# Pacing side work by measured prices, gate rows over 128 partitions, and a first norm at fixed places of TensorE's order

## The chip, the cores and the metric

The kernel runs on one core of a Trainium2 chip. A core has a matrix engine (TensorE, "PE" in the profile, with its weight loads as "PEld"), a vector engine (VectorE, "DVE"), a scalar engine (ScalarE, "ACT"), a general engine (GpSimd, "POOL") and an engine that here only issues transfers (SyncE, "SP"). Each runs its own queue of instructions in the order in which the compiled program has them, and waits on the others by semaphores. The metric is the device time of one execution in microseconds (us), as a median of several.

## The reference

One inference step of one layer of a hybrid decoder, in fp32, for 256 prompt tokens and 8 cached single-token requests ("sample" tokens), 264 columns in all. Cut to what matters:

```python
def layer(x, ...):                                  # D_MODEL 2048
    xn = rmsnorm(x, g_mix)
    z = xn @ w_in                                   # x part and gate part of rg, q, k, v, o, two gate rows per head
    # recurrent group (rg): conv, two block-diagonal gates, linear scan, gelu gate, norm
    xr, conv_new = causal_conv(z[..., :1024], ...)
    r, ig = sigmoid(block_diag(xr, ...)), sigmoid(block_diag(xr, ...))
    log_a = -8.0 * r * softplus(-lam)
    h = associative_scan(a = exp(log_a), bx = sqrt(1 - exp(2 * log_a)) * ig * xr)
    y_rg = rmsnorm(h * gelu(z_gate), g_rg_out)
    # mLSTM group: 4 heads, dk 128, dv 256, input gate logi and forget gate logf per head and token
    h_ml, C_new, n_new, m_new = mlstm(q, k, v, logi, logf, C0, n0, m0)
    y_ml = rmsnorm(h_ml, g_ml_out) * sigmoid(z_o)
    x = x + concat([y_rg, y_ml]) @ w_out
    # cross attention: 4 heads of 512 over 256 memory tokens
    xq = rmsnorm(x, g_xa) @ w_xa_q
    x = x + (softmax(xq @ mk.T * 512 ** -0.5) @ mv) @ w_xa_o
    xf = rmsnorm(x, g_ffn)                          # SwiGLU, 5632 wide
    return x + (silu(xf @ w_ffn_gate) * (xf @ w_ffn_up)) @ w_ffn_down
```

The prompt's memory keys and values are computed here from a normalised memory; the 8 sample tokens each have their own cached keys and values and their own mLSTM state, which are read from memory, used and, for the state, written back. The outputs are the normalised activations and all new states.

## The kernel before

Tokens lie along the free dimension (264 columns), features on the 128 partitions in chunks. The big products are made in three single-pass matmuls per chunk: activations and weights are each split into a high part in a rounded format and a remainder, and high x high, high x low and low x high are summed (`mm3`). The weights come in pieces of 2048 columns; each piece is one *step* of PE, 48 matmuls of 128x264. A list `steps` holds them in order: 0 to 3 the first bank pass over the input projection, 4 to 7 the rest of rg's x part, 8 the gate rows (`pe_if`), 9 to 16 q and k, 17 to 24 v, 25 to 32 rg's gate part, 33 to 40 o, 41 to 56 `w_out`, 57 to 72 `w_q`, 73 to 104 memory keys and values head by head, 105 to 120 `w_o`, then the feed-forward part. Each step has a source, a matmul function, an evacuation function and a list of names that it needs.

For every step the weights are split by a copy on ACT and a subtraction on DVE, per half of 1024 columns (`split_half`); four split buffers hold two steps, so a split starts when the matmuls of two steps earlier have read their half. The PSUM banks for the steps' results are four ("mm"), and four others ("ax") serve everything else.

All other work (norms, the rg recurrence, the mLSTM, the cached attention) is written as Python generators that are emitted between steps. The loop over the steps (before: lines 1299 to 1343) emits in this order: at some steps the end of a generator is forced (`finish`); the evacuation of the step before (`pend`), at raised priority; the split of the next step's weights; the step's matmuls; and then side generators through `pump(pe.clock + SLACK)`, SLACK being 0.5. The engines are wrapped in an object that adds a price to a clock for every instruction emitted (`price_dve`, `price_act`, `price_pe`, lines 64 to 77). `pump` lets a generator emit as long as the priced DVE and ACT clocks are both below the limit; a generator yields after small portions, and `yield STEP` gives up its turn for this step. A generator of priority below zero is run to its end with high priority. So the prices decide how much side work stands between two steps on each engine. A scheduler of the language then settles the final order on each engine, apart from stretches that are marked as manual.

Names that the change and the prediction touch:

- `norm_x`, the first norm's sums, reciprocal root and spreading over the partitions; `rstd` is its result. Before, it is a side generator of priority -1 that is started after step 3; its end is forced before step 5, and the result of step 4 stays unevacuated until then.
- `rg_gen` (from line 479): the recurrence; before it is started ahead of step 5.
- `evac_if` and `ml_gates` (lines 575 to 638): the gate rows of four heads, on partitions 0 to 3 of seven row tiles `R(0)` to `R(6)`. Their sums and maxima are spread over all partitions by matmuls against columns of the identity, `ident[0:4, h:h+1]`; five blocks of 128 columns are transposed.
- `ml_prompt` (from 665): the decay matrix of each head, which starts with one such spreading matmul over 256 columns.
- `ml_sample` (from 754): the state update of the sample tokens in 32 groups (4 heads, 8 requests): two ACT copies, one DVE `scalar_tensor_tensor` of 128x256 and two of 128x128 that accumulate. `bcs` holds its factors.
- `evac_o` (856): evacuation of the o steps, which forces `ml_sample` and the heads to their end; `ml_norm` (820) makes the mLSTM's norm.
- `rg_out` (541): norm and split of rg's result. `mem_gen`: the memory norm and its split.
- the cached attention ("dk" and "dv", 32 pairs of a key and a value tile): per pair three dot products on DVE, a sum over partitions by way of POOL and PE, an Exp, and four accumulating products on DVE. The first `w_o` step needs them, and the attention of head 2, finished.

Of the kernel before, what the change touches and what calls it, by code (L numbers as in the profile page):

```python
# [17 lines left out]
P = 128  # L18
D = 2048
KC = D // P  # L20
T = 256
# [42 lines left out]
def price_dve(name, n, a, k):  # L64
    fast = name in ("tensor_scalar", "tensor_copy", "tensor_single_scalar", "memset")
    if name == "tensor_reduce":
        n = int(np.prod(a[1].shape[1:]))
    return 0.07 + n * (0.00052 if fast else 0.0066 if name == "reciprocal" else 0.00104)


def price_act(name, n, a, k):
    return 0.12 + n * 0.00083


def price_pe(name, n, a, k):
    passes = 1 if name == "transpose" or a[1].dtype == F32R else 4
    return passes * n * 0.00042 + 0.003


@with_exitstack  # L80
def layer_kernel(ctx: ExitStack, tc, xT, memT, vec, wrg, w_in, w_out, w_q, w_k, w_v, w_o,
# [150 lines left out]
    def mm3(ps, a, b, start, stop):  # L232
        ah, al = a
        bh, bl = b
        pe.matmul(ps, ah, bh, start=start, stop=False)
        pe.matmul(ps, ah, bl, start=False, stop=False)
        pe.matmul(ps, al, bh, start=False, stop=stop)
# [20 lines left out]
    def side(g, prio=0):  # L258
        x = Gen(g, prio)
        gens.append(x)  # L260
        gens.sort(key=lambda q: q.prio)
        return x
# [12 lines left out]
    def finish(cond):  # L275

        for _ in range(10000):
            if cond():
                return
            pump(1e12)  # L280
        raise RuntimeError("side work does not end")
# [293 lines left out]
    def evac_if(ps):  # L575
        R = Arr(7)
        ml["R"] = R
        li, u, a, b = (R(j)[0:4] for j in range(4))
        act.activation(a, ps[64:68, :N], AF.Copy)
        act.activation(b, ps[96:100, :N], AF.Copy)  # L580
        dve.tensor_add(li, ps[0:4, :N], a)
        dve.tensor_add(u, ps[32:36, :N], b)
        dve.tensor_mul(li, li, rstd[0:4, :])
        dve.tensor_mul(u, u, rstd[0:4, :])
        dve.tensor_scalar(li, li, V("bi")[0:4], None, op0=OP.add)
        dve.tensor_scalar(u, u, V("bf")[0:4], None, op0=OP.add)
        ml["gates"] = side(ml_gates(), 1)
# [6 lines left out]
    def ml_gates():  # L594
        R = ml["R"]
        li, u, e, lf, b, g, M = (R(j)[0:4] for j in range(7))
        yield STEP
        dve.scalar_tensor_tensor(e, u, -1.0, u, op0=OP.mult, op1=OP.min)
        act.activation(e, e, AF.Exp)
        yield 0.4  # L600
        log1p(lf, e)
        yield 6.0
        dve.tensor_scalar(u, u, 0.0, None, op0=OP.min)
        dve.tensor_sub(lf, u, lf)

        one = ones[0:4, 0:1].to_broadcast([4, T])
        dve.tensor_tensor_scan(b[:, :T], one, lf[:, :T], 0.0, op0=OP.mult, op1=OP.add)
        dve.tensor_sub(g[:, :T], li[:, :T], b[:, :T])
        dve.tensor_tensor_scan(M[:, :T], g[:, :T], g[:, :T], 0.0, op0=OP.max, op1=OP.max)
        dve.tensor_add(b[:, :T], b[:, :T], M[:, :T])  # L610
        dve.tensor_scalar(M[:, :T], M[:, :T], -1.0, None, op0=OP.mult)
        dve.tensor_copy(mrow[:, 0:1], b[:, T - 1: T])

        s = slice(T, N)
        dve.tensor_add(lf[:, s], lf[:, s], V("m0", 0, 8)[0:4])
        dve.tensor_max(b[:, s], lf[:, s], li[:, s])
        dve.tensor_copy(mrow[:, 1:], b[:, s])
        x16 = e[:, 0:16]
        dve.tensor_sub(x16[:, 0:8], lf[:, s], b[:, s])
        dve.tensor_sub(x16[:, 8:16], li[:, s], b[:, s])  # L620
        act.activation(x16, x16, AF.Exp)
        pool_e.dma_start(o_m, mrow)
        yield 3.0
        yield STEP
        yield STEP
        ps = bank("ax")
        for h in range(H):
            pe.matmul(ps[:, h * 16: h * 16 + 16], ident[0:4, h: h + 1].to_broadcast([4, P]), x16,
                      start=True, stop=True)
        i4 = ident[0:4, 0:4]  # L630
        for j in range(2):
            pe.transpose(ps[:, 64 + 4 * j: 68 + 4 * j], g[:, j * P: j * P + P], i4)
        for j, w0 in enumerate(WIN):
            pe.transpose(ps[:, 72 + 4 * j: 76 + 4 * j], b[:, w0: w0 + P], i4)
        act.activation(bcs, ps[:, 0:64].rearrange("p (h j) -> p h j", j=16), AF.Copy)
        act.activation(gcol, ps[:, 64:72].rearrange("p (j h) -> p j h", h=H), AF.Copy)
        act.activation(emc, ps[:, 72:84], AF.Exp, scale=-1.0)
        yield 0.1
# [26 lines left out]
    def ml_prompt():  # L665
        qk = ml["qk"]
        yield STEP
        kt = B([P, 2, H, P])
        for tb in range(2):
            ps = bank("ax")  # L670
            for h in range(H):
                pe.transpose(ps[:, h * P: h * P + P], qk(4 + h)[:, tb * P: tb * P + P], ident)
            act.activation(kt[:, tb].rearrange("p h d -> p (h d)"), ps, AF.Copy)
            yield STEP
        while "gates" not in ml or not ml["gates"].done:
            yield STEP
        R = ml["R"]
        M = R(6)[0:4, :T]
        for h in range(H):
            sel = ident[0:4, h: h + 1].to_broadcast([4, P])  # L680
            bc = bank("ax")
            pe.matmul(bc[:, :T], sel, M, start=True, stop=True)
            sps = bank("ax")
            q, k = qk(h), qk(4 + h)
            pe.matmul(sps[:, 0:256], k[:, 0:P], q[:, 0:T], start=True, stop=True)
            pe.matmul(sps[:, 256:384], k[:, P:T], q[:, P:T], start=True, stop=True)
            w = B([P, 1024])
            E, Pm, kw = w[:, 0:384], w[:, 384:768], w[:, 768:1024]
            ml["w", h] = (Pm, kw)
            yield STEP  # L690
            dve.tensor_scalar(E[:, 0:256], bc[:, 0:T], gcol[:, 0, h: h + 1], 0.0, op0=OP.add, op1=OP.min)
            dve.tensor_scalar(E[:, 256:384], bc[:, P:T], gcol[:, 1, h: h + 1], 0.0, op0=OP.add, op1=OP.min)
            act.activation(E, E, AF.Exp)
            dve.tensor_mul(E[:, 0:128], E[:, 0:128], mask)
            dve.tensor_mul(E[:, 256:384], E[:, 256:384], mask)
            dve.tensor_mul(Pm, sps[:, 0:384], E)
            act.activation(kw[:, 0:P], kt[:, 0, h, :], AF.Copy, scale=E[:, 255:256])
            act.activation(kw[:, P:T], kt[:, 1, h, :], AF.Copy, scale=E[:, 383:384])
            yield 1.0
            ml["pn"] = h + 1  # L700
# [167 lines left out]
    def proj(src, rhs, evac, cols=2048, n=N, need=()):  # L868

        def f(i):  # L870
            ps = bank()
            w = W(i)
            nch = cols // P
            for c in range(nch):
                mm3(ps[:, :n], w(c), rhs(c), c == 0, c == nch - 1)
            return ps
        steps.append((src, cols, f, evac, need))
# [418 lines left out]
        split_half(0, 1)  # L1296

    pend = []
    for i, (src, cols, pef, evf, need) in enumerate(steps):
        if i > 1:  # L1300
            load_piece(i + LD - 1)
        if i == 5:
            finish(lambda: fn.done)
            st["rg"] = side(rg_gen(), 0)
        for q in need:
            if q in st:
                finish(lambda: st[q].done)
        if i != 4:
            with tc.high_priority(300):
                for e, x in pend:  # L1310
                    e(x)
            pend = []
        now = pe.clock
        dve.clock, act.clock = max(dve.clock, now), max(act.clock, now)
        split_half(i + LS, 0)
        if i + LS < len(steps) and steps[i + LS][1] > 1024:
            split_half(i + LS, 1)
        ps = pef(i)
        if 1 <= i < 4:
            with tc.issue_after(st["split"].ins):  # L1320
                for c in range(4 * i if i > 1 else 0, 4 * i + 4):
                    sumsq(acc_x, xres[:, c, :], c == 0)
        if i == 3:
            fn = side(norm_x(), -1)
        if evf is not None:
            pend.append((evf, ps))
        if i == 0:
            for c in range(0, 4, 2):
                load_x(sp, 12 + c, 14 + c)
                load_first(3, c)  # L1330
                load_first(3, c + 1)
        else:
            load_piece(i + LD)
        pump(pe.clock + SLACK)
        if i == 24:
            ml["ng"] = side(ml_norm(), 6)
        if i == 40:
            st["memg"] = side(mem_gen(), 7)
# [113 lines left out]
```

## Time and profile before

| | us |
|---|---|
| median of 3 runs | 1552.53 (1551.74 to 1553.06) |
| span of the profiled execution | 1548.1 |
| PE busy in it | 1533.5 (99%) |
| DVE busy | 1055.5 (68%) |
| ACT busy | 784.0 (51%) |
| POOL busy | 123.7 (8%) |

The page of the profile gives for one execution the busy time of each engine, the chain of work that ended last, and groups of instructions. A group's row has line, engine, operation, output and inputs, sizes, count, then busy time and the mean of one in ns, and the idle time ahead of them with what ended it. Line 60 is the wrapper through which every engine call goes, so most rows carry L60 and are told apart by their tiles: `w` are split weights, `raw` the loaded ones, `mm` and `ax` PSUM banks, `t`, `lt` and `B` work tiles. In a timeline a row is the start, the duration of a run of like instructions, the engine, and in brackets the idle time before it and what released it; runs overlap a little because matmuls are pipelined. In a table by windows, each window has the busy time and count of each engine, then the granted TensorE clock as a fraction, the share of the transfer engines and GB/s.

### The profile page before, as it was taken

To read this page: it belongs to the slowest core of one execution; us is meant where nothing else is said; L and a number is where in the kernel's file an instruction comes from. 1 tells how busy PE (TensorE), PEld (TensorE's weight loads), DVE (VectorE), ACT (ScalarE), POOL (GpSimd) and SP (SyncE) were. 2 spreads that over 40 slices of the span, in tenths; PEclk is the share of its full clock that TensorE was granted. 3 is DMA by queue.
4 is the path that set the end of the run, shared out by engine and by line. 5 is a ranking of instruction groups with operands and counts; after the bars stand their busy time and mean duration, and the time that the engine had idled before them with its cause. 6 is when DMAs were issued, how large, how long until landed. Compare 5 with 4: busy or idle time off the path is not lost.

```text
span 1548.1 us, 30188 instructions
## 1 busy us (share of the span) xinstructions
PE 1533.5 (99%) x12098; PEld 1500.4 (97%) x12098; DVE 1055.5 (68%) x2026; ACT 784.0 (51%) x1255; POOL 123.7 (8%) x190
## 2 busy tenths in 40 slices
PE   9999999999999999999999999999999999999997
PEld 9999999999999888899999999999999999999997
DVE  7886888796699989876665555445555545555554
ACT  7565775665455656555444444333444433444463
POOL 0001210000134333310000000000000000000000
PEclk9999999999999999999999999999999999999999
DMA  9556984547789887855555555555555555555563
GB/s 301 187 164 204 309 288 171 193 158 259 251 294 356 320 296 252 309 181 180 187 177 181 186 181 188 181 185 183 183 185 181 186 183 186 180 188 178 163 181 107
DMA packets 99757, 326.01 MB, mean 211 GB/s; under 512 B 10945, under 2 KB 19825, under 8 KB 99617
## 3 DMA queue, kind: packets, MB, share of 16 engines
q1 hardware_dynamic: 83472, 269.57, 52.1%
q0 software_dynamic: 15136, 53.16, 9.7%
q8 instruction: 94, 1.54, 0.4%
q10 hardware_dynamic: 1008, 1.36, 0.3%
q14 instruction: 47, 0.38, 0.1%
HBM read 312.78 MB, written 11.28 MB: 209 GB/s over the span
## 4 chain that ended last, share of the span: by engine, by line
PE 96%; DVE 2%; ACT 1%; DMA 0%; issue 0%; SPq 0%; DVEq 0%; ACTq 0%
PE mm L60 90%; PE ax L60 6%; DVE B L60 1%; ACT B L60 0%; DVE w L60 0%; DMA raw<-w_in 0%; ACT w L60 0%; ACT L60 0%; DVE xres L60 0%; DVE c L60 0%; ACT rstd L60 0%; SPq L1278 0%; DVE acc_x L60 0%; DVEq L1429 0%; ACT t L60 0%
## 5 line engine op out<-in xcount | busy, mean ns | idle before, releaser
L60 PE MATMUL mm<-B,w 128*128 128x264 f32 (+1 forms) x10960 | 1365.3, 285 | 4.1 <-DVE w L60 2.4
L60 PEld LDWEIGHTS mm<-B,w 128*128 128x128 f32 x10960 | 1338.6, 188 | 16.4 <-DVE w L60 2.8
L60 ACT ACTIVATE w<-raw 128x1024 fp32r<-128x1024 f32 (+1 forms) x522 | 537.9, 1031 | 654.6 <-PE mm L60 447.3
L60 DVE TENSOR_TENSOR w<-raw,w 128x1024 fp32r<-128x1024 f32 (+1 forms) x522 | 623.1, 1195 | 357.0 <-ACT w L60 356.0
L60 PE MATMUL mm<-w,B 128*128 128x512 f32 x384 | 91.0, 391 | 0.0
L60 PEld LDWEIGHTS mm<-w,B 128*128 128x128 f32 x384 | 70.7, 188 | 14.3
L60 DVE TENSOR_TENSOR t<-mm,rstd 128x264 f32<-128x264 f32 x104 | 44.8, 431 | 44.2 <-PE mm L60 43.5
L1344 POOL TENSOR_TENSOR B<-B,rstd 128x264 f32<-128x264 f32 x4 | 2.8, 736 | 855.5 <-ACT rstd L60 855.5
L60 DVE TENSOR_TENSOR xres<-xres,mm 128x264 f32<-128x264 f32 (+1 forms) x81 | 34.2, 423 | 38.9 <-PE mm L60 38.9
L60 DVE SCALAR_TENSOR_TENSOR B<-B,dw 128x256 f32<-128x256 f32 x128 | 55.6, 488 | 3.9 <-ACT dw L60 3.9
L60 DVE SCALAR_TENSOR_TENSOR dw<-B,qsm,dw 128x256 f32<-128x256 f32 x96 | 49.6, 525 | 0.4
L60 PE MATMUL ax<-B,B 128*128 128x256 f32 (+3 forms) x288 | 48.1, 308 | 0.0
L60 PEld LDWEIGHTS ax<-B,B 128*128 128x128 f32 x288 | 40.8, 190 | 3.2 <-ACT w L60 0.3
L1031 POOL TENSOR_TENSOR ds<-dw,ds 128x256 fp32r<-128x256 f32 x32 | 34.6, 1085 | 108.1 <-ACT ds L60 108.1
L60 ACT ACTIVATE B<-xres,vecs 128x264 fp32r<-128x264 f32 (+1 forms) x64 | 32.1, 502 | 1.5 <-DVE xres L60 1.0
L60 ACT ACTIVATE t<-xres 128x264 f32<-128x264 f32 (+2 forms) x61 | 24.0, 410 | 15.2 <-DVE xres L60 15.2
L1020 POOL DMA_DIRECT2D B<-kcT x32 | 17.3, 542 | 140.1 <-DVE B L60 131.0
L60 ACT ACTIVATE B<-t 128x264 fp32r<-128x264 f32 (+1 forms) x60 | 24.2, 409 | 4.6 <-DVE t L60 4.3
L60 DVE TENSOR_TENSOR acc_x<-acc_x,t 128x264 f32<-128x264 f32 x59 | 25.1, 426 | 1.0 <-ACT t L60 0.5
L60 DVE SCALAR_TENSOR_TENSOR B<-xres,vecs,B 128x264 fp32r<-128x264 f32 x48 | 23.4, 487 | 3.1 <-ACT B L60 3.1
L60 ACT ACTIVATE t<-t 128x264 f32<-128x264 f32 (+1 forms) x61 | 24.8, 406 | 1.3 <-DVE t L60 1.2
L60 ACT ACTIVATE dw<-B,qsm 128x256 f32<-128x256 f32 x32 | 16.2, 507 | 17.4 <-DVE B L60 10.7
(152 smaller groups left out, 666.9 us busy)
## 6 DMA issues: line engine op xcount, KB each, us to landing
raw<-w_gu SPq DMA_DIRECT2D x176, 512.0 KB, 3.5
raw<-w_d SPq DMA_DIRECT2D x80, 512.0 KB, 3.5
raw<-w_in SPq DMA_DIRECT2D x74, 512.0 KB, 4.6
raw<-w_out SPq DMA_DIRECT2D x32, 512.0 KB, 4.0
B<-kcT POOLq DMA_DIRECT2D x32, 512.0 KB, 8.1
raw<-w_q SPq DMA_DIRECT2D x32, 512.0 KB, 3.7
B<-vcT POOLq DMA_DIRECT2D x32, 512.0 KB, 8.5
raw<-w_k SPq DMA_DIRECT2D x32, 512.0 KB, 6.8
```

Of the source, the lines that this page charges most:

```text
L60: return f(*a, **k)
L1020: pool_e.dma_start(kc, kcT[h, b])
L1031: pool_e.tensor_sub(ws[:, 1], acc, ws[:, 0].bitcast(F32))
L1344: e.tensor_mul(st["y"](c), st["y"](c), r)
```

## The change

Three parts. The prices become dearer and finer: a DVE instruction gets a fixed 0.15 or 0.21 us instead of 0.07 and more if it accumulates or scans, an ACT one 0.18 or 0.27 instead of 0.12 and more if it accumulates, a PE transpose and a small matmul their own fixed figures. The gate rows are used over all 128 partitions: two of the row tiles are set to zero first, the identity's whole column stands where four rows of it stood, and five transposes become matmuls against four columns of the identity. The first norm no longer is a side generator: its two parts are emitted at the third chunk of steps 5 and 6, PE's order is manual from step 4 to the end of step 6, the results of steps 4 to 6 stay unevacuated until step 7, and `rg_gen` starts at step 7.

```diff
-    return 0.07 + n * (0.00052 if fast else 0.0066 if name == "reciprocal" else 0.00104)
+    rate = {"reciprocal": 0.0066, "tensor_tensor_scan": 0.00208}.get(name, 0.00052 if fast else 0.00104)
+    fixed = 0.21 if name == "scalar_tensor_tensor" else 0.15
+    return fixed + n * rate + (0.08 if "accum_out" in k else 0.0)

 def price_act(name, n, a, k):
-    return 0.12 + n * 0.00083
+    by_column = not isinstance(k.get("scale", 1.0), (int, float))
+    return (0.27 if by_column else 0.18) + n * 0.00085 + (0.2 if "accum_out" in k else 0.0)

 def price_pe(name, n, a, k):
-    passes = 1 if name == "transpose" or a[1].dtype == F32R else 4
-    return passes * n * 0.00042 + 0.003
+    if name == "transpose":
+        return 0.11
+    if a[1].dtype == F32R:
+        return 0.0045 + n * 0.000437
+    return max(0.224, 0.005 + n * 0.00167)
...
     def evac_if(ps):
         R = Arr(7)
         ml["R"] = R
+        for q in range(2):
+            pool_e.memset(R.tile(q), 0.0)
...
         for h in range(H):
-            pe.matmul(ps[:, h * 16: h * 16 + 16], ident[0:4, h: h + 1].to_broadcast([4, P]), x16,
+            pe.matmul(ps[:, h * 16: h * 16 + 16], ident[:, h: h + 1].to_broadcast([P, P]), R(2)[:, 0:16],
                       start=True, stop=True)
-        i4 = ident[0:4, 0:4]
-        for j in range(2):
-            pe.transpose(ps[:, 64 + 4 * j: 68 + 4 * j], g[:, j * P: j * P + P], i4)
-        for j, w0 in enumerate(WIN):
-            pe.transpose(ps[:, 72 + 4 * j: 76 + 4 * j], b[:, w0: w0 + P], i4)
+        for o, x, at in ((64, R(5), WIN[:2]), (72, R(4), WIN)):
+            for j, w0 in enumerate(at):
+                pe.matmul(ps[:, o + 4 * j: o + 4 * j + 4], x[:, w0: w0 + P], ident[:, 0:4], start=True, stop=True)
...
-        M = R(6)[0:4, :T]
+        M = R(6)[:, :T]
         for h in range(H):
-            sel = ident[0:4, h: h + 1].to_broadcast([4, P])
+            sel = ident[:, h: h + 1].to_broadcast([P, P])
...
             for c in range(nch):
+                if i in (5, 6) and c == 2:
+                    with tc.high_priority():
+                        st["rstd_x"].run(lambda: True)
                 mm3(ps[:, :n], w(c), rhs(c), c == 0, c == nch - 1)
...
+    kept = ExitStack()
     for i, (src, cols, pef, evf, need) in enumerate(steps):
...
-        if i == 5:
-            finish(lambda: fn.done)
+        if i == 7:
             st["rg"] = side(rg_gen(), 0)
...
-        if i != 4:
+        if not 4 <= i < 7:
             with tc.high_priority(300):
                 for e, x in pend:
                     e(x)
...
+        if i == 4:
+            kept.enter_context(tc.manual_schedule(engines={mybir.EngineType.PE}))
         ps = pef(i)
+        if i == 6:
+            kept.close()
...
         if i == 3:
-            fn = side(norm_x(), -1)
+            st["rstd_x"] = Gen(norm_x())
```

## The prediction

> **What bounds the kernel now.** I read the page first, then TensorE's (PE's) waits, then its timeline around each wait, the granted clock there, and last the groups of VectorE (DVE) and ScalarE (ACT).
>
> ```profile
> PE 1533.5 (99%) x12098; PEld 1500.4 (97%) x12098; DVE 1055.5 (68%) x2026; ACT 784.0 (51%) x1255; POOL 123.7 (8%) x190
> PE 96%; DVE 2%; ACT 1%; DMA 0%; issue 0%; SPq 0%; DVEq 0%; ACTq 0%
> ```
>
> PE is busy for all but 14.6 of 1548.1 us and is 96% of the chain that ended last. So no pacing of DVE and ACT work can bring more than PE's few waits, and any work of theirs that becomes late is paid in full. The page's execution spans 1548.1 us; the median of the runs, 1552.53, lies 4.4 above it, and I add that constant to whatever I sum.
>
> ```profile
> PE mm L60 <- DVE w L60: 2.4, 2, 1.5
> PE mm L60 <- DVE B L60: 1.7, 1, 1.7
> ```
>
> ```profile
> 48.07 0.73 PE L60 MATMUL ax<-ident,c 128*128 128x128 f32 x6
> 48.66 0.73 PE L60 MATMUL mm<-B,w 128*128 128x264 f32 x4
> 51.12 12.00 PE L60 MATMUL mm<-B,w 128*128 128x264 f32 x98 [1.73 <-DVE B L60]
> ...
> 119.18 0.81 PE L60 MATMUL ax<-ident,B 4*128 4x4 f32 x5
> 121.52 8.68 PE L60 MATMUL mm<-B,w 128*128 128x264 f32 x57 [1.53 <-DVE w L60]
> ...
> 258.35 59.42 PE L60 MATMUL mm<-B,w 128*128 128x264 f32 x494
> ...
> 344.91 5.32 PE L60 MATMUL mm<-B,w 128*128 128x264 f32 x42 [0.82 <-DVE w L60]
> ```
>
> ```profile
> 118.00:122.00 4.00, 2.47 (x20) 2.05 (x20) 4.00 (x9) 3.60 (x7) 0.00 (x0) 1.00 0.01 2
> 122.00:126.00 4.00, 4.00 (x23) 4.00 (x22) 4.00 (x6) 0.61 (x2) 0.00 (x0) 0.57 0.59 180
> ```
>
> The three waits are 1.73 (first norm), 1.53 (recurrent block, "rg") and 0.82 us (memory norm). The windows (their seventh number is the granted clock) show what the second one drags behind it: 0.57 from 122 to 126 us, about 3.4 us at half speed. 57 matmuls take 8.68 us there; at 59.42/494 = 0.120 us each they would take 6.9, so about 1.7 us go to the clock.
>
> **First norm (steps 4 to 7).** The factor's work is fixed inside steps 5 and 6, and the results of steps 4 to 6 are scaled only before step 7.
>
> ```profile
> 49.26 1.31 DVE L60 TENSOR_TENSOR B<-ax,rstd 128x256 f32<-128x256 f32 x6 [2.03 <-ACT rstd L60]
> 50.48 0.89 DVE L60 TENSOR_TENSOR B<-mm,rstd 128x256 f32<-128x256 f32 x4
> ```
>
> Before, PE spreads the factor over the partitions at 48.07, because its place is there, and scaling ends at 51.37 (50.48 + 0.89), 3.3 us later; step 7, ready for its first matmul at 49.39, waits for it. In the changed order the spread stands within step 6, some 4 us earlier, so scaling ends near 47.3, 2 us before it is needed. The wait goes: -1.7 (0 if the factor's small DVE work in between takes 2 us longer). Next to be late are the weight splits of steps 8 to 10, which I count 1 to 2 us ahead. rg starting two steps later costs nothing by itself; what it pushes along is summed below.
>
> **Gate rows over 128 partitions.** Two POOL memsets are added; POOL is busy 8% and they stand a step ahead of their readers: nothing.
>
> ```profile
> 117.52 0.51 PE L60 MATMUL mm<-B,w 128*128 128x264 f32 x2
> 117.96 0.61 PE L60 MATMUL ax<-B,ident 4*128 4x16 f32 x4
> 118.42 0.38 PE L60 MATMUL ax<-ident,B 4*128 4x4 f32 x4
> ...
> 150.51 0.69 PE L60 MATMUL ax<-B,ident 4*128 4x256 f32 x2
> 151.14 0.92 PE L60 MATMUL ax<-B,B 128*128 128x256 f32 x4
> 151.89 0.60 PE L60 MATMUL ax<-ident,B 128*128 128x128 f32 x4
> ...
> 167.22 1.47 PE L60 MATMUL ax<-B,B 128*128 128x256 f32 x8
> 168.45 2.40 PE L60 MATMUL mm<-B,w 128*128 128x264 f32 x18
> ```
>
> From 150.51 to 151.89 are 1.38 us for one broadcast from 4 rows (256 columns) and a full-height pair (256 and 128 columns). Two such pairs alone take 167.22 to 168.45, 1.23 us, so 0.62 a pair and, at two thirds of it, 0.41 for 256 columns: 1.03 in all. By starts 0.35 is the price of four rows; by ends, where the matmul behind also loses some, I get 0.385. Four heads: -1.5. In the cluster at 117 to 120 the same happens at each change of height: two weight matmuls take 117.52 to 117.96, 0.44 instead of 0.24. Over its three changes that makes 0.6 to save, and five transposes that become matmuls of two passes cost about as much: nothing. Together -1.5 (0 to -2.3).
>
> [...]
>
> **Prices.** Side generators run until their priced DVE and ACT time passes PE's, and what is unfinished is forced out where a step needs it. Dearer prices on DVE and ACT mean fewer side instructions a step. That is good at 120 us (the 29-instruction rg block ahead of a split is broken up: -1.5 for the wait, -1.7 for the clock) and leaves the work of the cached tokens unfinished at two forced ends. I followed the changed program's order on each engine to both.
>
> ```profile
> L60 DVE TENSOR_TENSOR w<-raw,w 128x1024 fp32r<-128x1024 f32 x488 | 599.8, 1230 | 352.7 <-ACT w L60 351.8
> L60 DVE SCALAR_TENSOR_TENSOR B<-B,dw 128x256 f32<-128x256 f32 x128 | 55.6, 488 | 3.9 <-ACT dw L60 3.9
> L60 DVE SCALAR_TENSOR_TENSOR dw<-B,qsm,dw 128x256 f32<-128x256 f32 x96 | 49.6, 525 | 0.4
> L60 DVE TENSOR_TENSOR acc_x<-acc_x,t 128x264 f32<-128x264 f32 x59 | 25.1, 426 | 1.0 <-ACT t L60 0.5
> L60 DVE TENSOR_REDUCE dw<-ax 128x1 f32<-128x256 f32 x32 | 13.2, 415 | 2.5 <-PE ax L60 2.4
> L60 DVE DVE_READ_ACCUMULATOR B<-B,dw 128x1 f32 x128 | 10.0, 78 | 0.0
> ```
>
> ```profile
> L60 ACT ACT_TABLE_LOAD x12 | 15.4, 1283 | 2.8 <-issue 2.2 <-DVE t L60 0.4
> L60 ACT ACTIVATE w<-raw 128x1024 fp32r<-128x1024 f32 x488 | 516.7, 1060 | 640.4 <-PE mm L60 436.2 <-issue 189.7 <-ACT B L60 10.0
> L60 ACT ACTIVATE dw<-ax,dw 128x256 f32<-128x256 f32 x32 | 15.0, 470 | 13.4 <-DVE dw L60 13.2 <-POOL ds L1031 0.2
> L60 ACT ACTIVATION_READ_ACCUMULATOR dw<-ax,dw 128x1 f32 x32 | 6.3, 197 | 0.0
> ```
>
> *Forced end 1, behind step 37 (about 250 us).* The mLSTM state update of the cached tokens is 32 groups, one 128x256 and two accumulating 128x128 operations each.
>
> ```profile
> L60 DVE SCALAR_TENSOR_TENSOR B<-B,bcs,t x32: 470/478/485, 147.6 to 220.7; 128x256 f32<-128x256 f32 x32
> ```
>
> ```profile
> 207.83 0.48 DVE L60 SCALAR_TENSOR_TENSOR B<-B,bcs,t 128x256 f32<-128x256 f32 x1
> ...
> 208.89 1.22 DVE L60 TENSOR_TENSOR w<-raw,w 128x1024 fp32r<-128x1024 f32 x1
> ```
>
> Before, they run from 147.6 to 220.7, spread between splits, and end some 25 us ahead of step 37's end. In the changed order, counted in the matmul time that stands ahead of them, the gates come 20 us later, the groups start about 30 us later, and output evacuation forces the end of the generator: ten groups and two extra accumulations stand in one piece on DVE, behind the split of step 39's second half and ahead of the evacuations of steps 34 to 37. That split's ACT copy takes over the buffer that step 37's last matmul reads, so the piece cannot start before step 37 is over. What PE issues next needs its end: the mLSTM norm's sums over three further adds, and step 38 a bank that those evacuations free. From step 37's last matmul: copy 1.06, split 1.23, ten groups at 208.89 - 207.83 = 1.06 are 10.6, two accumulations 0.7, three adds at 0.35 (0.426 less the overlap of 0.08 at which such rows follow each other) 1.05: 14.6 us with PE idle. The normalised rg rows stand just ahead and can make DVE up to 3 us late; I take +15 (13 to 18).
>
> *Forced end 2, start of w_o (about 680 us).* Cross attention over the cached tokens has 32 pairs of key and value tiles.
>
> ```profile
> 670.41 0.42 DVE L60 SCALAR_TENSOR_TENSOR B<-B,dw 128x256 f32<-128x256 f32 x1
> ...
> 670.75 0.42 DVE L60 SCALAR_TENSOR_TENSOR B<-B,dw 128x256 f32<-128x256 f32 x1
> ...
> 673.17 0.20 DVE L60 RECIPROCAL ssm<-ssm 128x8 f32<-128x8 f32 x1
> ...
> 675.02 0.39 DVE L60 TENSOR_TENSOR osm<-osm,ssm 128x8 f32<-128x8 f32 x4
> ```
>
> Before, the last pair ends at 673.17 and its outcome at 675.4, just as w_o's first four steps run out of other columns. In the changed order the last 61 DVE instructions of this work, with four whole pairs and the accumulations of two more, follow the last split that PE can use. They are 24 accumulations at 0.34 (670.41 to 670.75), 8.3; twelve dot products at 0.45 to 0.525, about 6; six reductions 2.3; the end 2.8: 19.4 us. Each pair also goes DVE, ACT, POOL, PE, DVE, ACT, DVE, and the Exp with its read (0.47 + 0.20) is exposed several times; I count 5.5 us of waits. PE has 5.0 us of matmuls of its own to set against these 24.9: +20. Without waits it would be 14.4; at the group's mean of 0.488 + 0.078 an accumulation, 5.4 more, about 26.
>
> *Query projection (about 340 to 390 us).* The memory norm's products and splits move from 327-345 beside the cross-attention norm. The wait of 0.82 at 344.91 goes; a bank of the first query step is freed later. No row shows that wait; between nothing and ten further instructions of 0.426 (the row of the adds), 4 us, I take +2, since about half of them stand ahead of it.
>
> *Tables.* The changed order loads six more ACT tables, 1.283 us each, and ACT is busy 51%: nothing, or 1.3 at a deadline.
>
> **Clock.** Both pieces leave PE idle far longer than the 1.53 us that went with the half-speed stretch at 122, so I add its 1.7 us twice: +3.4 (0 to 6.8, were each stretch twice as long). [...]
>
> **Sum.** -1.7 (norm) -3.2 (rg wait and clock) -1.5 (gate rows) -0.8 (memory norm) +15 +20 +2 +3.4 = +33.2. Against the profiled execution, 1548.1 + 33.2 = 1581.3 us of span; with the constant 4.4, 1585.7 us.
>
> **Rivals.** *A, one piece is hidden* (0.17): at w_o the remaining matmuls of the attention's values or a DVE that runs ahead take most of the 20. Speaking for it: DVE is only 68% busy, so that it may enter this end early. Against: four pairs are chained through PE itself. 1585.7 less 17 is about 1569; it decides if the waits at w_o stay below 5 us. *B, faster* (0.05): the pieces are long but PE does not wait there, because their readers stand later in its order than I read. Then only the savings and the query wait count: 1552.5 - 7.2 + 2 = 1547. It decides if DVE is through both pieces within the 5 us of matmuls that PE holds in reserve. Against it stand two dependences on PE's own matmuls. *C, larger* (0.06): splits behind the pieces come late as well, one copy and one split, 2.3 us, for two halves at either end, 9 in all, and each half-speed stretch is twice as long: 18 + 26 + 4 + 9 - 7.2 + 7 = +57, 1609. *D, the pacing does not do what it says* (0.04): the rg block still blocks its split, and the 3.2 us stay: 1589 with both pieces.
>
> **Numbers.** Forecast 0.68 with 1574 to 1597.5 for itself: 13 + 14.4 + 0 - 8 + 2 = +21 (1574) at the low end, 18 + 26 + 4 - 7 + 4 = +45 (1597.5) at the high end. The range reaches to A: 1566 to 1600. Faster by over 0.2% (3.1 us, about what can be told from no change here) 0.05; within it 0.02, if savings and a single short wait cancel; slower 0.93.
>
> **What would show it.** Right: no wait at step 7, none near 120 and a clock of 1.0 there; one wait of about 15 us by step 38's sums on DVE's accumulations at about 245 to 262, its DVE share full; waits adding up to some 20 us at the first w_o steps, on reductions and outcomes of the cached tokens; clock about 0.5 behind both. Wrong: PE's waits shorter than 10 us in all, or a wait at 40 to 60 that the moved factor makes.

## The result, and the profile after

The changed kernel takes 1596.55 us, the kernel before 1552.44: a ratio of 1.0282 (95% interval 1.0269 to 1.0294). It is 44 us slower. The forecast was 1585.7, with a range to 1600.

The page of the changed kernel, the lines that answer to those shown of before:

```profile
span 1592.6 us, 30180 instructions
...
PE 1544.7 (97%) x12103; PEld 1510.4 (95%) x12103; DVE 1052.9 (66%) x2026; ACT 794.9 (50%) x1261; POOL 126.6 (8%) x192
...
PEclk9999997899999999997999999999999999999999
```

The span grew by 44.5 us. No engine has more work worth the name: DVE's busy time fell by 2.6 us. PE is "busy" 11 us longer with five more matmul records, so that part of its matmuls became slower, and the other 33 us are idle. The granted clock dips at the seventh and eighth and at the nineteenth of 40 slices. TensorE's waits (engine, line, releaser, then total, count and longest):

```profile
PE ax L60 <- DVE B L60: 16.4, 1, 16.4
PE ax L60 <- ACT ds L60: 11.3, 3, 6.1
PE mm L60 <- ACT B L60: 3.1, 2, 2.7
PE mm L60 <- DVE w L60: 1.7, 3, 0.7
PE mm L60 <- DVE qsm L60: 1.4, 1, 1.4
```

Before, the list was 2.4 and 1.7 us. Now there is one wait of 16.4, and a family of waits on the cached attention (`ds`). The timeline shows where they stand, and what became of the places that the change meant to mend:

```profile
44.02 0.73 PE L60 MATMUL ax<-ident,c 128*128 128x128 f32 x6
44.60 15.60 PE L60 MATMUL mm<-B,w 128*128 128x264 f32 x128
...
142.69 15.73 PE L60 MATMUL mm<-B,w 128*128 128x264 f32 x116 [0.67 <-DVE w L60]
...
164.47 0.59 PE L60 MATMUL ax<-B,ident 128*128 128x256 f32 x2
164.91 0.82 PE L60 MATMUL ax<-B,B 128*128 128x256 f32 x4
165.56 0.60 PE L60 MATMUL ax<-ident,B 128*128 128x128 f32 x4
...
276.21 3.97 PE L60 MATMUL ax<-ones,B 128*128 128x1 f32 x18 [16.40 <-DVE B L60]
...
424.87 11.76 PE L60 MATMUL mm<-B,w 128*128 128x264 f32 x96 [1.42 <-DVE qsm L60]
...
726.89 0.58 PE L60 MATMUL ax<-ds,onesr 128*128 128x256 f32 x1 [5.02 <-ACT ds L60]
...
735.31 0.58 PE L60 MATMUL ax<-ds,onesr 128*128 128x256 f32 x1 [6.12 <-ACT ds L60]
...
744.53 5.71 PE L60 MATMUL mm<-B,w 128*128 128x264 f32 x45 [2.70 <-ACT B L60]
```

The spread of the factor moved from 48.07 to 44.02, and PE runs through from there: the wait of 1.73 us at step 7 is gone. The wait in the rg block is 0.67 instead of 1.53. The broadcast of a gate row with the pair behind it takes 164.47 to 165.56, 1.09 us, where it took 1.38. These three small gains are there; the half-clock stretch behind the rg block is not gone, as the windows below show. Against the gains stand the two forced ends, at 276 and at 709 to 745, and they cost far more.

The windows behind the rg block and around both ends (busy time of PE, PEld, DVE, ACT and POOL, then the granted clock):

```profile
140.00:144.00 4.00, 3.33 (x24) 3.09 (x24) 4.00 (x8) 3.70 (x7) 0.00 (x0) 0.86 0.06 23
144.00:148.00 4.00, 4.00 (x27) 4.00 (x26) 3.82 (x10) 1.67 (x4) 0.55 (x1) 0.71 0.91 290
260.00:276.00 16.00, 0.00 (x0) 0.00 (x0) 15.24 (x67) 9.82 (x30) 1.59 (x3) 0.57 0.43 156
276.00:280.00 4.00, 3.79 (x18) 3.82 (x19) 2.45 (x8) 2.03 (x6) 0.53 (x1) 0.50 0.32 131
284.00:288.00 4.00, 4.00 (x19) 4.00 (x20) 2.32 (x14) 1.01 (x1) 0.53 (x1) 0.50 0.39 133
288.00:290.00 2.00, 2.00 (x12) 2.00 (x11) 1.23 (x1) 0.04 (x1) 0.00 (x0) 0.58 0.00 0
723.00:740.00 17.00, 5.95 (x19) 4.56 (x20) 13.58 (x53) 5.66 (x15) 3.29 (x4) 0.51 0.21 83
```

In 16 us DVE works 15.24 us while PE issues nothing. When PE resumes it runs at half clock until 289.7, 13.5 us long: half of that, about 6.7 us, is lost beyond what the wait itself shows. DVE's rows at the two ends of that stretch:

```profile
263.34 1.22 DVE L60 TENSOR_TENSOR w<-raw,w 128x1024 fp32r<-128x1024 f32 x1
...
274.57 0.48 DVE L60 SCALAR_TENSOR_TENSOR B<-B,bcs,t 128x256 f32<-128x256 f32 x1
...
275.64 1.11 DVE L60 TENSOR_TENSOR B<-B,t 128x264 f32<-128x264 f32 x3
276.67 1.45 DVE L60 TENSOR_TENSOR t<-mm,rstd 128x264 f32<-128x264 f32 x4
```

The split of step 39's second half at 263.34, the ten groups to 275.64, the three adds, and only then the four evacuations, in one row.

### The profile page after: what moved, and what is told of

It is laid out like the page before. It is cut to its first block, busy times and chain, and to the rows that moved or that the text cites. A ratio compares the mean times of both kernels' runs of the same rounds, so it can differ in the third digit from the quotient of the medians.

```text
span 1592.6 us, 30180 instructions
## 1 busy us (share of the span) xinstructions
PE 1544.7 (97%) x12103; PEld 1510.4 (95%) x12103; DVE 1052.9 (66%) x2026; ACT 794.9 (50%) x1261; POOL 126.6 (8%) x192
## 4 chain that ended last, share of the span: by engine, by line
PE 53%; DVE 1%; ACT 0%; issue 0%; DVEq 0%; ACTq 0%
PE mm L60 52%; DVE B L60 0%; PE ax L60 0%; DVE dw L60 0%; DVE c L60 0%; ACT dw L60 0%; ACT ds L60 0%; DVEq L1442 0%; ACT t L60 0%; DVE xres L60 0%; ACT B L60 0%; ACT c L60 0%; DVE ssm L60 0%; DVE osm L60 0%; ACTq L60 0%
## 5 line engine op out<-in xcount | busy, mean ns | idle before, releaser
L60 DVE TENSOR_TENSOR t<-mm,rstd 128x264 f32<-128x264 f32 x104 | 44.5, 432 | 44.2 <-PE mm L60 44.1
L60 DVE SCALAR_TENSOR_TENSOR B<-B,dw 128x256 f32<-128x256 f32 x128 | 49.9, 445 | 5.6 <-ACT dw L60 5.5
L60 PE MATMUL ax<-ds,onesr 128*128 128x256 f32 x64 | 17.7, 314 | 12.2 <-ACT ds L60 11.3
L60 PEld LDWEIGHTS ax<-ds,onesr 128*128 128x128 f32 x64 | 12.0, 202 | 14.7 <-ACT ds L60 12.1
```

What stands on the lines that cost most here:

```text
L60: return f(*a, **k)
```

## The experiments

Theory P: VectorE's dearer price alone leaves the side work over, and both waits follow from that. Rivals: the later start of rg (third part), the gate rows, or ScalarE's price. Each run's own kernel before, on the same chip, has a median between 1550.8 and 1551.8 us; ratios go against that.

**Prices of before, the other two parts kept.**

```diff
-    rate = {...}; fixed = 0.21 if name == "scalar_tensor_tensor" else 0.15   # and price_act, price_pe
+    return 0.07 + n * (0.00052 if fast else 0.0066 if name == "reciprocal" else 0.00104)
```

> The changed kernel with all three price functions of before, so gate rows and first norm alone. Theory P (the loss is the prices' alone): both waits, 16.4 us at 276 and the ones at 709 to 745, are gone; 1552.4 - 1.7 (step 7) - 1.5 (gate rows) = 1549, between 1547 and 1551, and a wait of 1 to 2 us on a split in the rg block stays, with its 3.4 us at half clock. Rival N (the later start of rg and of what follows it, from step 7, leaves the sample groups unfinished): a wait of at least 5 us at the mLSTM norm's sums, 1560 or more.

Measured: 1557.18 us, 1.0036 (1.0025 to 1.0047). Both long waits are gone, which bears out theory P for some 38 of the 44 us (1.0282 over 1.0036). But the kernel is slower than before, where a gain of 3.2 us was expected. Its timeline there:

```profile
130.11 0.52 PE L60 MATMUL mm<-B,w 128*128 128x264 f32 x2 [1.25 <-ACT w L60]
132.01 0.55 PE L60 MATMUL ax<-ident,B 128*128 128x128 f32 x3 [1.05 <-DVE B L60]
134.45 15.49 PE L60 MATMUL mm<-B,w 128*128 128x264 f32 x116 [1.65 <-DVE w L60]
...
235.91 4.32 PE L60 MATMUL mm<-B,w 128*128 128x264 f32 x21 [3.57 <-DVE t L60]
```

The wait of 1.65 answers to the 1.53 of before; the other three, 5.9 us together, are new. Rival N's wait at the mLSTM norm's sums did not come. It was right only in that the other two parts make work late, elsewhere and for less.

**New prices alone, on the kernel before.**

```diff
-def price_dve(...): return 0.07 + n * (...)          # and price_act, price_pe of before
+def price_dve(...): return fixed + n * rate + (0.08 if "accum_out" in k else 0.0)
```

> The kernel before with only the three price functions of the changed one. Theory P: both forced ends are there, and the savings of the other two parts are not: 1596.5 + 1.7 + 1.5 = about 1600 (1594 to 1604), waits of 14 to 17 us by 250 to 280 and some 20 at 700 to 750. Rival N: with rg at step 5 the sample groups end in time; only the second piece is left: about 1575.

Measured: 1603.56 us, 1.033 (1.0313 to 1.0347). Both forced ends come with rg at step 5 as well:

```profile
PE ax L60 <- DVE B L60: 14.0, 1, 14.0
PE ax L60 <- ACT ds L60: 11.3, 3, 6.1
```

So the prices are enough, and no other part is needed. The losses do not add: 3.3% by the prices and 0.36% by the other parts make 2.8% together.

**Only VectorE's price back to the old one.**

```diff
 def price_dve(name, n, a, k):
-    return fixed + n * rate + (0.08 if "accum_out" in k else 0.0)
+    return 0.07 + n * (0.00052 if fast else 0.0066 if name == "reciprocal" else 0.00104)
```

> The changed kernel with VectorE's price of before and the new ScalarE and TensorE prices. Theory V (VectorE's price alone makes the pieces): both long waits gone, 1547 to 1551. Rival (ScalarE's dearer price holds the generators back as well): at least one long wait left, 1565 or more.

Measured: 1554.07 us, 1.0017 (1.0007 to 1.0026). No wait is longer than 3.6 us. So the pieces need VectorE's new price; ScalarE's and TensorE's without it do not make them. Whether VectorE's would make them beside the old prices of the two others, no run shows. The time is above the expected 1547 to 1551, and the wait of 3.57 us near 240 is here too; the run with a ring of its own, below, bears on it.

**VectorE's new price less the overlap.**

```diff
-    fixed = 0.21 if name == "scalar_tensor_tensor" else 0.15
-    return fixed + n * rate + (0.08 if "accum_out" in k else 0.0)
+    fixed = 0.07
+    return fixed + n * rate
```

> The changed kernel with VectorE's new price less what consecutive rows overlap: a fixed 0.07 us for all, no surcharge for accumulation; the scan's doubled rate is kept. Theory O (a row's duration counts about 0.08 us, and an accumulation's read, that the next instruction overlaps; the price of before was the spacing of rows): no long wait, and since scans are priced in full the split in the rg block is in time too, 1549 - 3.2 = about 1546 (1544 to 1549). Rival (doubling the scan's rate or the later gates suffice to leave work over): a wait of 5 us or more near 250 to 280, 1556 or more.

Measured: 1552.51 us, 1.0005 (0.9996 to 1.0015). No forced piece is left, with the scan still at its doubled rate: theory O's forecast for the 44 us came true. The further gain of 3.2 us did not come: a split's wait of 0.78 us near 130 stays and the 3.57 near 243 with it. The trace has no half clock near 130, but one stretch of 3.4 us each at 243.5 and 257.1: 68 matmuls from 130.47 take 8.43 us, 68 from 243.22 take 9.94, and 21 from 256.26 take 4.25. What is wrong with the new price can be read in rows shown above. Three adds of 128x264 begin at 275.64 and the next row at 276.67: 0.343 us each, while a row of this kind lasts 0.426. The old price of such an add is 0.07 + 264 x 0.00104 = 0.345, the new one 0.425. For such rows the old price was their spacing, the new one is their duration, and durations overlap. An accumulating 128x256 product is the worst case: 0.488 + 0.078 by its two rows, 0.556 by the new price, and 0.34 from one to the next, as by the old price (0.07 + 256 x 0.00104 = 0.336). For the scan the old price was not the spacing: it gives 0.336 for 256 columns, and in the trace of before the row behind such a scan begins 0.60 us after it, as the doubled rate has it (0.07 + 256 x 0.00208 = 0.602).

**One piece at a time.** The price was switched inside the loop over the steps.

```diff
     for i, (src, cols, pef, evf, need) in enumerate(steps):
+        dve._price = price_dve_old if i <= 40 else price_dve      # the other run: if i > 40
```

> The changed kernel with VectorE's price of before up to step 40, its new price from step 41 on. If the two pieces are separate: the first goes with its clock (16.4 + 6.2) and the small wait of the run with the old VectorE price stays (3.6 and its clock 1.7): 1596.5 - 22.6 + 5.3 = about 1579, the waits at the first w_o steps unchanged near 23 us. If the delay of the first piece makes part of the second: 1565 or less.

> The changed kernel with VectorE's new price up to step 40 and that of before from step 41 on. If the pieces are separate: the first stays with 16.4 us and its half clock, the second goes: 1596.5 - 23.1 = about 1573.5, or 2 less without the wait at the query projection. If the first makes the second: over 1580.

Measured: 1577.67 us, 1.0163 (1.0141 to 1.0185), with the old price up to step 40, and 1572.27 us, 1.0137 (1.0111 to 1.0163), with it from step 41. Waits of the first, then of the second:

```profile
PE ax L60 <- ACT ds L60: 11.0, 3, 6.1
PE mm L60 <- DVE t L60: 4.3, 2, 3.6
```

```profile
PE ax L60 <- DVE B L60: 16.4, 1, 16.4
PE mm L60 <- DVE qsm L60: 2.3, 1, 2.3
```

Each piece goes without touching the other. Against 43.8 us for the whole (1.0282 of 1552.4), the first piece is worth 43.8 - 25.3 = 18.5 us, beyond the small wait of 3.6 that stays in its place, and the second 43.8 - 21.3 = 22.5. Together 41; the old VectorE price throughout brings 43.8 - 2.6 = 41.2. By the two intervals each of the two figures is good to about 4 us, so that the agreement to 0.2 is partly luck. The pieces are separate and, within that, account for the loss.

**PE kept busy in the first wait.** 68 fp32 matmuls were added behind step 37; they write an unused part of that step's bank, and PE's order is manual in that step, to keep them there.

```diff
         ps = pef(i)
+        if i == 37:
+            idle, was = ps[:, 384:512], pe.clock
+            for _ in range(68):
+                pe.matmul(idle, ones, ones, start=True, stop=True)
+            pe.clock = was
```

> The changed kernel with 68 further fp32 matmuls of 128x128 columns on TensorE behind step 37's last matmul, into an unused part of that step's bank: about 15 us of work inside the wait of 16.4. Theory K (idleness costs the clock, and the 13.5 us at half speed behind the wait lose over 6 us): the wait shrinks to 1 to 2 us, the clock stays 1.0, and the time falls by about 6 from 1596.5 to 1590.5, although work is added. Rival (the half clock comes from what runs behind the wait, the sums of one column): 1596.5, half clock at the same place.

Measured: 1595.19 us, 1.028 (1.0262 to 1.0297), which cannot be told from the changed kernel. The place itself, in its timeline and windows:

```profile
259.77 15.35 PE L60 MATMUL mm<-ones 128*128 128x128 f32 x136
276.33 2.14 PE L60 MATMUL ax<-ones,B 128*128 128x1 f32 x18 [1.21 <-DVE B L60]
...
421.94 13.31 PE L60 MATMUL mm<-B,w 128*128 128x264 f32 x96 [1.42 <-DVE qsm L60]
```

```profile
262.00:276.00 14.00, 13.12 (x118) 12.93 (x116) 13.24 (x60) 8.16 (x27) 1.59 (x3) 1.00 0.43 152
280.00:286.00 6.00, 6.00 (x29) 6.00 (x29) 3.02 (x15) 1.06 (x1) 0.53 (x1) 0.50 0.61 176
286.00:290.00 4.00, 4.00 (x36) 4.00 (x35) 2.20 (x6) 0.44 (x1) 0.00 (x0) 0.95 0.41 135
```

The clock stays at 1.00 through the wait and is halved all the same from 279.5 to 286.4, behind the sums of one column. Half-speed work falls from 13.5 to 6.8 us, about half of what theory K expected: the work behind it, 24 matmuls against the identity, begins at 287.65 instead of 290.61, 3.0 us earlier. All of that is lost again elsewhere. The 96 matmuls behind the query wait take 13.31 us here and 11.76 in the changed kernel, behind the same wait of 1.42. At the second piece half clock comes back once more, from 743.7 to 747.2: 127 matmuls from 743.20 take 17.08 us, where 128 from 744.53 take 15.66 in the changed kernel. Both reach 760.2 to 760.3. The rival has its part of the truth, and how often half clock comes is not a constant of the program: the eleven executions of the kernel with the gate rows and the scan priced in full have mean granted clocks from 0.994 to 0.998.

**The third part alone, and the second alone.**

```diff
-        if i == 5:
-            finish(lambda: fn.done)
+        if i == 7:                         # norm at steps 5 and 6, banks of 4 to 6 kept: as in the change
```

> The kernel before with only the third part (first norm at fixed places, rg from step 7). Theory N2 (the later rg start costs more than the wait of step 7 that it removes): about 1.5 us above the run with all old prices, so 1.004 to 1.005 of the time before: waits of 3 to 4 us on splits and transposes in the rg block near 130, and 3.6 us near 236 on an evacuation that stands behind the sample groups; none at step 7. Rival (it was the gate rows that cost there): 0.998 to 0.999, those waits gone.

```diff
-            sel = ident[0:4, h: h + 1].to_broadcast([4, P])
+            sel = ident[:, h: h + 1].to_broadcast([P, P])      # and the rest of the gate rows
```

> The kernel before with only the gate rows over 128 partitions. Theory G (a change between 4 and 128 rows costs TensorE about 0.2 us each time): 1.5 us less, 0.9985 to 0.9995 of the time before, the spreading matmuls at 0.38 instead of 0.43 us a record and 1.09 instead of 1.38 us with the pair behind them. Rival (height does not matter, five matmuls replace transposes): 1.000 to 1.0005.

The norm alone: 1556.98 us, 1.0034 (1.0021 to 1.0047). The waits near 130 and the one of 3.57 at 236 are there without the gate rows, and none stands at step 7:

```profile
133.69 15.58 PE L60 MATMUL mm<-B,w 128*128 128x264 f32 x116 [1.66 <-DVE w L60]
236.17 4.04 PE L60 MATMUL mm<-B,w 128*128 128x264 f32 x20 [3.57 <-DVE t L60]
```

The third part costs more than the 1.73 us of step 7 bring. These waits stand in rg's own block and at an evacuation behind the sample groups, which points at rg's start two steps later; no run moves that start without the held banks and PE's manual order. The gate rows alone: 1551.51 us, 1.0000 (0.9992 to 1.0009). The matmuls are shorter (a broadcast and the pair behind it take 152.03 to 153.11, 1.08 us, where they took 1.38), but PE, ahead by that much, waits for the decay matrices and values that DVE makes (this trace is of an execution of 1554.86 us, 3.3 above the run's median, and has two more stretches at half clock than the trace of before: 98 matmuls from 51.19 take 13.55 us, where 98 from 51.12 took 12.00, and 57 from 232.02 take 8.66):

```profile
167.91 0.66 PE L60 MATMUL ax<-ident,B 128*128 128x128 f32 x4 [0.50 <-DVE B L60]
169.72 1.58 PE L60 MATMUL ax<-B,B 128*128 128x256 f32 x8 [1.15 <-DVE B L60]
...
181.05 1.57 PE L60 MATMUL ax<-B,B 128*128 128x256 f32 x8 [0.57 <-DVE B L60]
```

**Gate rows and the scan priced in full.**

```diff
-    return 0.07 + n * (0.00052 if fast else 0.0066 if name == "reciprocal" else 0.00104)
+    return 0.07 + n * (0.00052 if fast else 0.0066 if name == "reciprocal"
+                       else 0.00228 if name == "tensor_tensor_scan" else 0.00104)
```

> The kernel before with the gate rows over 128 partitions and VectorE's price of before in which only the scan is charged its row's length (0.00228 us an element instead of 0.00104). If scans too cheap by half are what puts the rg block ahead of its split: the wait of 1.5 us near 120 and its half clock go, 1.5 + 3.2 us less, 0.997 of the time before. If the wait comes from elsewhere in the block, or the sample groups end too late for it (they end one and a half steps later in its order): 0.999 to 1.002.

Measured: 1552.34 us, 1.0003 (0.9994 to 1.0012). The wait by the rg block shrank only from 1.5 to 1.3 us. Scans too cheap are not what puts the block ahead of its split.

**A ring of their own for two evacuations, and everything mended together.** Both runs stand on the changed kernel: the first has VectorE's price of before, the second VectorE's price by spacing and 1.0 us more lead for side work in steps 9 to 36. Cut to the ring:

```diff
+    def ztmp():
+        return sb.tile([P, N], F32, tag="z", bufs=2, name=nm("z"))
-    NB, NT, NL, NFL = 26, 6, 3, 2
+    NB, NT, NL, NFL = 26, 4, 3, 2
-            z = tmp()                       # in evac_rgg and evac_o
+            z = ztmp()
```

> The changed kernel with VectorE's price of before, and with two buffers of their own for the products that evacuate rg's gate part and o (taken from the six of the ring t, which the sample groups use too, so that four are left). Theory R (the wait of 3.6 us near 240 is an evacuation that gets its buffer only behind sample groups issued before it): that wait and the 0.7 before it go, with the half clock behind them (two stretches, 3.4 us): 1554.1 - 4.3 - 3.4 = about 1546.5, 0.996 to 0.998 of the time before. Rival (the evacuation is late by its place among the groups whatever its buffer): wait unchanged, 1.001 to 1.002.

> The changed kernel with VectorE's price by the spacing of rows (as in the run of that name), the evacuations' own two buffers, and 1.0 us more lead for side work in steps 9 to 36. In its order the sample groups end at step 37 as in the kernel before. If gains of the parts survive once nothing is late: no wait at step 7, none over 1 us up to 400, 0.995 to 0.998 of the time before. Rival (small waits move elsewhere as they did with the gate rows alone): 0.999 to 1.001.

The first: 1548.44 us, 0.9981 (0.9972 to 0.9990). By its interval it is faster than the kernel before, by 3 us. The wait of 3.57 is gone from its list:

```profile
PE mm L60 <- DVE w L60: 1.6, 2, 0.8
PE ax L60 <- ACT w L60: 1.4, 1, 1.4
```

Theory R holds: an evacuation that shares its buffers with the sample groups is queued behind them, and PE then lacks the bank. 5.6 us were gained against the run with the old VectorE price, 7.7 expected. The second run: 1549.57 us, 0.9997 (0.9987 to 1.0008). It has one wait of note, where PE transposes values for the heads:

```profile
182.31 0.66 PE L60 MATMUL ax<-ident,B 128*128 128x128 f32 x4 [2.21 <-DVE B L60]
```

Its rival was right: another small wait opened. Whether the longer lead or the other price opened it, no run shows.

## Why the prediction was right, point by point

Direction, mechanism and both places were right, from the order of the changed program and the rows of before. By its steps:

- **First norm, -1.7.** The wait is gone. What the step missed is the price of the later rg start. "Costs nothing by itself" was wrong: the third part alone costs 5.3 us net of its gain. In the changed kernel the wait of 3.57 at the evacuation is not there; that the larger delay of the sample groups hides it is a reading, not shown.
- **Gate rows, -1.5.** At the place 0.29 us per head by starts, where 0.35 had been worked out. As a sum it failed when alone: 1.0000. That PE then waits for DVE, 2.2 us in the three waits shown above, was not considered. The records did get shorter: a spreading matmul of 256 columns takes 0.378 us a record over 128 rows in the changed kernel, 0.426 over 4 before.
- **rg wait and clock, -3.2.** The wait went from 1.53 to 0.67, and a half-speed stretch stayed behind it: 8.68 us for 57 matmuls before, and in the changed kernel a clock of 0.86 and 0.71 over 140 to 148. So about -0.9, and the sign that was named for it, no wait at the block and a clock of 1.0 there, did not come.
- **Forced end 1, +15.** The wait measured 16.4. The working by groups was right, ten of them; 1.8 us come on top of the 14.6 worked out, within the 3 us that were allowed for a late DVE. The split at 263.34 begins 2.4 us after its copy, which starts with step 37's end at 259.89 and takes 1.06.
- **Forced end 2, +20.** The waits between 709 and 745 add up to 17 us. With its share of the clock the piece is worth 22.5 us, good to 4, by the run that takes it away; 20 and 1.7 had been put for it.
- **Query projection, +2.** Waits of 0.68 and 1.42, 2.1; the 0.82 at 344.91 is gone.
- **Clock, +3.4.** This is the term that was mis-sized. It put one stretch of 3.4 us behind each piece, as in the trace of before. Behind the first PE ran at half speed for 13.5 us, four such stretches, and lost about 6.7 us instead of 1.7. Behind the second the windows show 5.95 us of work at half speed, so about 3.0 lost, which the 22.5 above contains. Together that is past the 6.8 put as the term's upper end.

With -1.7, -0.9, -1.2, -0.8, 16.4, 6.7, 22.5 and 2.1 and a new wait of 0.8 at 240 the steps make 43.9 of the 44.1 us measured. That is closer than the 4 us of the second piece's figure allow to claim. The forecast fell 11 us short: 5 for the clock of the first piece, 2.3 for the rg block, the rest spread over the two waits, the second piece and the new wait at 240.

Rival A (one piece hidden) fell: neither is. B fell with it. C was nearer with its longer half-speed stretches, still short of the four behind the first piece; its 9 us of late splits did not come, the waits on splits around w_o are 2.2 us. D was half right: the rg block did not hold its split for long, but the clock still fell.

## What to carry to other kernels

A planner that paces work by priced time needs the spacing of instructions, not their durations as a trace prints them: here 0.34 us against 0.43 to 0.57, and some 41 us followed. Where side work has forced ends, look at what is still left at each of them when any price rises, and what stands behind it; here the dear price collected its error at the deadlines. A small saving on the bounding engine is only worth what the next engine can follow (1.0000 for the gate rows alone), and evacuations should not draw their buffers from a ring that side work also fills (a wait of 3.57 us here).

## What the runs showed of the hardware

The half-speed stretches read in the traces last 3.41 us from 122.31 before and from 142.91 in the changed kernel, 6.8 from 279.5 in the run with the added matmuls, 17.07 from 723.17 and 27.31 from 262.37 in the changed kernel: one, two, five and eight times 3.41. Two of them follow on waits far shorter than that: 1.53 us at 120 before and 0.67 at 142.69 after, both next to a cluster of matmuls of 16 and 4 columns. And the one behind the first forced end did not end with the first 3.4 us of resumed work: in the changed kernel PE resumes at 276.21 and full speed comes at 289.7. There and in the run with added matmuls, PE's first work after the wait were sums of one column. Wide matmuls, but for eleven in between, began at 283.74 in the one and at 281.05 in the other; full speed came at 289.7 and 286.4, 5.9 and 5.4 us later.

Stretches also begin without any wait. In the run with a ring of its own PE is busy throughout, and the clock halves behind such sums:

```profile
236.92 2.06 PE L60 MATMUL ax<-ones,B 128*128 128x1 f32 x18
...
239.53 0.72 PE L60 MATMUL ax<-ones,B 128*128 128x1 f32 x6
...
240.45 1.23 PE L60 MATMUL ax<-ones,acc_rg 128*128 128x1 f32 x6
241.53 10.32 PE L60 MATMUL mm<-B,w 128*128 128x264 f32 x62
```

```profile
240.50:247.30 6.80, 6.80 (x33) 6.80 (x33) 3.94 (x22) 1.37 (x2) 0.00 (x0) 0.50 0.82 327
```

The run with the gate rows alone has the same at 232.8, behind 24 sums at 229.42 and no wait: the 57 matmuls from 232.02 take 8.66 us, like the 57 of 8.68 behind the wait at 120 before. So a stretch came without idle time in these two places. Whether the single column of the sums has a part in it, no run shows, since none changed the columns alone. For the prediction it means that the clock term was tied to idle time alone, and stretches came without it as well. Neither a wait's length nor the sums alone decide whether a stretch follows. The same 1.42 us at the query projection drew one in the run with added matmuls (13.31 us for the 96 matmuls behind it) and none in the changed kernel (11.76), and the 24 sums at 226.07 before drew none (a granted clock of 1.00 from 227 to 235).
